# The second block's first feed-forward product, both token halves in seven products per 2x2x2 block

## The chip, the cores and the metric

The kernel runs on one core of a Trainium2 chip. The metric is device time in microseconds (us), from runs without a profiler; besides, one execution is recorded by the hardware profiler. Engines: TensorE (PE, with its weight loads PEld), VectorE (DVE), ScalarE (ACT), GpSimd (POOL), and SyncE (SP), which issues the DMAs.

## The reference

A trunk of two layers over 1024 tokens of width 1024, in float32. Each layer is a token mixer and a dense feed-forward block, each followed by a normalisation:

```
h = layer_norm(sqrt(2) * h + mixer(h))               # layer 0: RWKV-7, layer 1: S5 and a gate
h = layer_norm(sqrt(2) * h + square(relu(h @ w1)) @ w2)   # w1: 1024 x 4096, w2: 4096 x 1024
```

The S5 mixer is a diagonal complex state-space scan over all tokens; its output y goes through GELU and the gate z = y @ w_glu, z[:, :1024] * sigmoid(z[:, 1024:]).

## The kernel before

Activations are kept transposed: eight tiles of 128 features x 512 tokens for each half of the tokens, `hA` (first) and `hB` (second). A float32 product is done in three: each operand is split into a high part (fp32r, a cast on ScalarE) and the remainder (a subtraction on VectorE; `split`, L151 and L152), and high x high, high x low and low x high are added up in PSUM (`mm3`, issued at L197). Weights come by `wload` (L172): a raw tile of 256 KB by DMA (tag `wraw`, 2 buffers), split into `whi` and `wlo` (3 buffers each). PSUM tiles of products come from `psd` (tag `d`, 3 buffers).

The feed-forward block, `mlp`, treats the 4096 hidden features in 16 pairs of blocks of 128. `up(b)` computes a pair: for each of the two blocks 8 x 3 matmuls of 128x128 by 128x512, then ReLU on ScalarE (L985), the square on GpSimd (L986) and a split into `qbuf`. `down(b)` multiplies the pair by its rows of w2 (four weight tiles, 16 x 3 matmuls) and adds the eight results into h on VectorE (L1000 for the first pair, L1002 after). `up` runs one pair ahead of `down`. Each half has its own pass, so every weight is loaded and split once per half. In the last pass, the last TB = 2 pairs' `down` is done in two column halves, so that the last normalisation (`last_norm`) can start on one.

`layer_norm` sums over features with a matmul by a constant matrix, squares on ScalarE, adds on VectorE and GpSimd, and rescales. It uses temporary tiles of tags `la` and `m` (2 buffers each). `s5(H, h)` transposes its half, multiplies by tables to get the scan's inputs (`hb`), scans on VectorE and GpSimd (`advance`: L1232 to L1238, the groups 0 to 15 on VectorE, 16 to 31 on GpSimd where the step is long), multiplies by output tables (`tt`, `tcm`, tag `tab`, 4 buffers, loaded from DRAM), and writes y to DRAM through one buffer `yg`. `glu(H, h)` reads it back (`yload`, tag `m`), and does two products of 8 x 3 matmuls for each of eight feature tiles.

The order of the work: the program text gives each instruction a rising priority number, `rank(n)` sets it for a passage (smaller is more urgent; normalisations have 99000, S5 99300 and 99400, all else from 200000 up). A planner with a modelled time line then writes out the order on each engine. The passes stand in the program thus: feed-forward of layer 0 for hA; normalisation and S5 of hA; feed-forward of layer 0 for hB, with the gate of hA and its normalisation put in after INS3 = 12 pairs; normalisation and S5 of hB; feed-forward of layer 1 for hA, with the gate of hB and its normalisation put in after INS2 = 13 pairs; the last normalisation of hA and its store; feed-forward of layer 1 for hB, with the last normalisation.

The program's functions that the change touches, and their callers:

## Time and profile before

| | us |
|---|---|
| median of 3 runs | 2686.01 (2684.6 to 2688.53) |
| profiled execution, span from first to last instruction | 2674.1 |
| median less span | 11.9 |
| TensorE busy in the span | 2516.9 (94%) |
| VectorE, ScalarE, GpSimd busy | 1795.2, 1150.5, 578.8 |

The profile's rows name a line, an engine, an operation, and the output and inputs by tile name. Matmuls are pipelined: one of 128x512 is shown as some 390 ns long, but they start every 0.23 us in a dense stretch, so counts of matmuls over a stretch tell more than busy time. A few matmul records can be missing. In tables by stretch the columns are the stretch, its length, busy time and count for each engine, the granted TensorE clock (1.00 is full), the DMA engines' busy share and GB/s; in groups, the busy time and the mean of one in ns, then the idle time of the engine before them and what ended it.

### The profile page before, as it was taken

What the parts mean: (1) busy time and instruction counts of PE and PEld (TensorE: products, weight loads), DVE (VectorE), ACT (ScalarE), POOL (GpSimd) and SP (SyncE); (2) the same over time, 40 slices, a digit from 0 to 9 for tenths busy, and PEclk for the clock granted to TensorE, in tenths of its full rate; (3) what the DMA queues carried; (4) which work ended last, traced back from release to release, by engine and by line L of the source; (5) the groups of instructions that cost most, each with busy time, mean ns of one, the idle gap of its engine ahead of it and who ended that gap; (6) DMA issues with size and microseconds to landing.
All of it is one profiled execution on the core that took longest, in us unless ns stands there. A gap on an engine that the chain in (4) does not pass through costs nothing.

```text
span 2674.1 us, 44098 instructions
## 1 busy us (share of the span) xinstructions
PE 2516.9 (94%) x16768; PEld 2036.1 (76%) x16768; DVE 1795.2 (67%) x3140; ACT 1150.5 (43%) x2059; POOL 578.8 (22%) x484
## 2 busy tenths in 40 slices
PE   7899979999889999999998999999999999999997
PEld 5678757788667777777877788778778887788886
DVE  7367687487886867987586553675955536855556
ACT  7555565454454343344523332445233324533334
POOL 3121552342442122112121000121210001200001
PEclk9999889898889999999999999999999999999999
DMA  4765545663323334662436332234253322333333
GB/s 155 253 207 188 161 163 177 196 187 123 96 72 92 95 91 148 180 192 85 124 101 202 114 96 98 83 91 129 89 197 99 99 95 83 122 99 95 99 95 103
DMA packets 221397, 345.92 MB, mean 129 GB/s; under 512 B 21889, under 2 KB 83457, under 8 KB 221185
## 3 DMA queue, kind: packets, MB, share of 16 engines
q1 hardware_dynamic: 221184, 343.11, 41.4%
q8 instruction: 132, 2.16, 0.3%
q14 instruction: 81, 0.66, 0.1%
HBM read 279.06 MB, written 63.96 MB: 128 GB/s over the span
## 4 chain that ended last, share of the span: by engine, by line
PE 50%; DVE 13%; DMA 5%; issue 3%; ACT 2%; POOL 1%; SPq 0%; ACTq 0%; DVEq 0%; POOLq 0%
PE d L197 46%; DVE wlo L152 3%; DMA wraw<-in_mw_dram 2%; DMA s_y<-yg 1%; DVE hA L1002 1%; DMA yl<-s_y 1%; DVE t L1234 1%; DVE sq L887 1%; DVE hB L1002 1%; PE pbu L1222 1%; PE pu L1210 1%; DVE qbuf L152 1%; ACT whi L151 1%; DVE hb L1238 0%; POOL rl L986 0%
## 5 line engine op out<-in xcount | busy, mean ns | idle before, releaser
L151 ACT CAST whi<-wraw 128x512 fp32r<-128x512 f32 x668 | 413.7, 620 | 933.5 <-PE d L197 597.2
L152 DVE TENSOR_TENSOR wlo<-wraw,whi 128x512 fp32r<-128x512 f32 x668 | 500.9, 751 | 417.8 <-ACT whi L151 412.0
L197 PE MATMUL d<-qbuf,whi 128*128 128x512 f32 (+1 forms) x2112 | 655.8, 393 | 34.0 <-DVE hA L1002 14.1
L197 PEld LDWEIGHTS d<-qbuf,whi 128*128 128x128 f32 x2112 | 390.3, 190 | 132.0 <-DVE hA L1002 22.3
L197 PE MATMUL d<-qbuf,wlo 128*128 128x512 f32 (+1 forms) x1056 | 409.2, 390 | 9.2 <-DVE wlo L152 9.0
L197 PE MATMUL d<-oAh,whi 128*128 128x512 f32 (+1 forms) x960 | 385.3, 408 | 12.0 <-ACT ev L427 8.3
L986 POOL TENSOR_TENSOR rl<-rl 128x512 f32<-128x512 f32 x128 | 148.9, 1163 | 1135.3 <-ACT rl L985 1130.5
L197 PE MATMUL d<-oAl,whi 128*128 128x512 f32 (+1 forms) x960 | 380.9, 400 | 8.0 <-DVE oAl L152 8.0
L197 PE MATMUL d<-oAh,wlo 128*128 128x512 f32 (+1 forms) x960 | 381.9, 402 | 2.8 <-DMA wlo<-low 2.8
L197 PE MATMUL d<-oBh,whi 128*128 128x512 f32 x704 | 278.6, 396 | 1.9 <-ACT whi L151 1.9
L197 PE MATMUL d<-oBh,wlo 128*128 128x512 f32 x704 | 277.7, 395 | 1.9 <-DVE wlo L152 1.9
L197 PE MATMUL d<-oBl,whi 128*128 128x512 f32 x704 | 275.2, 391 | 0.0
L197 PEld LDWEIGHTS d<-qbuf,wlo 128*128 128x128 f32 x1056 | 200.7, 190 | 55.0 <-DVE wlo L152 13.5
L197 PEld LDWEIGHTS d<-oAh,whi 128*128 128x128 f32 (+1 forms) x960 | 183.4, 193 | 55.0 <-ACT ev L427 10.4
L197 PEld LDWEIGHTS d<-oAl,whi 128*128 128x128 f32 (+1 forms) x960 | 183.6, 193 | 46.3 <-DVE oAl L152 9.9
L197 PEld LDWEIGHTS d<-oAh,wlo 128*128 128x128 f32 (+1 forms) x960 | 183.2, 192 | 43.1 <-DMA wlo<-low 3.0
L1002 DVE TENSOR_TENSOR hB<-hB,d 128x512 f32<-128x512 f32 (+1 forms) x256 | 165.0, 652 | 62.0 <-PE d L197 59.3
L1002 DVE TENSOR_TENSOR hA<-hA,d 128x512 f32<-128x512 f32 x240 | 162.3, 684 | 53.0 <-PE d L197 50.4
L197 PEld LDWEIGHTS d<-oBh,wlo 128*128 128x128 f32 x704 | 132.2, 188 | 34.0 <-DVE wlo L152 3.2
L197 PEld LDWEIGHTS d<-oBh,whi 128*128 128x128 f32 x704 | 132.4, 188 | 30.2 <-ACT whi L151 2.9
L197 PEld LDWEIGHTS d<-oBl,whi 128*128 128x128 f32 x704 | 132.2, 188 | 29.3 <-issue 0.7
L152 DVE TENSOR_TENSOR qbuf<-rl,qbuf 128x512 fp32r<-128x512 f32 x128 | 96.5, 754 | 70.8 <-ACT qbuf L151 70.1
(365 smaller groups left out, 3629.7 us busy)
## 6 DMA issues: line engine op xcount, KB each, us to landing
wraw<-in_mw_dram SPq DMA_DIRECT2D x520, 256.0 KB, 2.7
wraw<-in_glu_dram SPq DMA_DIRECT2D x64, 256.0 KB, 2.6
low<-wlo SPq DMA_DIRECT2D x52, 256.0 KB, 2.8
wlo<-low SPq DMA_DIRECT2D x52, 256.0 KB, 3.6
wraw<-in_wk_dram SPq DMA_DIRECT2D x32, 256.0 KB, 3.2
wraw<-in_wr_dram SPq DMA_DIRECT2D x32, 256.0 KB, 3.8
wraw<-in_wv_dram SPq DMA_DIRECT2D x32, 256.0 KB, 4.6
yl<-s_y SPq DMA_DIRECT2D x32, 256.0 KB, 3.4
```

The lines of the kernel that those rows point to most:

```text
L151: S.copy(hi, src)
L152: (e or V).tensor_sub(lo, src, hi.bitcast(F32))
L197: bulk.append((PE.matmul(p, w, x, **kw).ins, x.shape[-1]))
L887: (G if k % 2 else V).tensor_add(sa[k % 2], sa[k % 2], q)
L986: G.tensor_mul(r, r, r)
L1002: V.tensor_add(z, z, p)
L1210: PE.matmul(p[64 * (1 - e) : 64 * (1 - e) + 64, g], u1[:, j, g].rearrange("p s c -> p (s c)"), sel[:, e], start=True, stop=True)
L1222: PE.matmul(p[qs, g2, ri], tb[:, g2, ri, qs], u[:, 2 * g2 + par], start=True, stop=True)
L1234: e.tensor_mul(t2[:, :, ri], x[:, :, 1 - ri], bw[:, l, g0:g1, ri : ri + 1].broadcast_to([128, g1 - g0, n]))
```

## The change

In layer 1 the two token halves are taken through 13 of the 16 pairs together. With K the two halves of the 1024 input features, M the two blocks of a pair and N the two token halves, a pair's first product is a 2x2x2 block product; Strassen's scheme (in Winograd's form) does it in seven products of 4 x 3 matmuls in place of eight. The token operands T1 to T4 are sums of quarters of hA and hB, made and split once, and kept in a new pool `jp`, which takes the space of S5's pool (closed after the second S5), and in buffers of `qbuf` and of hA's operands. The weight sums (s1, s2 and two more) are made for each pair on GpSimd from four raw tiles (two of tag `wraw`, two of tag `m`); the results are put together from PSUM on VectorE, ScalarE and GpSimd. `down` then uses each weight tile for both halves.

The first JB = 3 pairs are done for hA alone before that (`blocks`, the former body of `mlp`), and for hB alone after it, the last two of them with `down` in two column halves as before. The gate of hA is moved behind the whole of hB's feed-forward pass of layer 0, and the gate of hB follows it, ahead of all of layer 1's feed-forward work. Manual dependences hold the raw tiles of tag `m` back until the last token sum is done (`after`), and the first joint pair's tiles of tag `wraw` until the last weight load before them (`behind`). Nothing else of the computation changes.

```diff
 TB = 2
+JB = 3
...
             PE.transpose(out, x, idt)
 
+    behind = []
...
         for k0 in range(0, kt, step):
             kept = low.get((key, k0)) if key else None
             raw = wp.tile([128, step, n], F32, tag="wraw", name="wraw", bufs=2)
-            SP.dma_start(raw, src[:, k0 : k0 + step])
+            behind.append(SP.dma_start(raw, src[:, k0 : k0 + step]))
             hi = wp.tile([128, step, n], F32R, tag="whi", name="whi")
             lo = wp.tile([128, step, n], F32R, tag="wlo", name="wlo")
             nw[0] += 1
...
             hs.append(h)
         return hs
 
-    def mlp(i, H, h, xo):
-        nb = 32 // KB2
+    def blocks(i, h, xo, qbuf):
+
         nw = 512 // KB2
         qs = {}
 
...
                 split(r, qt[:, 0], qt[:, 1])
                 qs[b].append((qt[:, 0], qt[:, 1]))
 
-        def down(b, cs=slice(0, HT)):
+        def down(b, first=False, cs=slice(0, HT)):
             for n2 in range(C // nw):
                 w = wload(A["mw2"][i, b, n2], KB2, nw)
                 for n in range(nw // 128):
...
                     dense(p, [(x[:, n * 128 : (n + 1) * 128], y[:, n * 128 : (n + 1) * 128]) for x, y in w],
                           [(x[:, cs], y[:, cs]) for x, y in qs[b]])
                     z = h[n2 * (nw // 128) + n][:, cs]
-                    if b == 0:
+                    if first:
                         V.scalar_tensor_tensor(z, z, ALPHA, p, op0=ALU.mult, op1=ALU.add)
                     else:
                         V.tensor_add(z, z, p)
+
+        return up, down
+
+    def mlp(i, h, xo, qbuf):
+
+        nb = 32 // KB2
+        up, down = blocks(i, h, xo, qbuf)
         up(0)
-        last = TB if i == 1 and H == 1 else 0
-        for b in range(nb - last):
+        for b in range(nb):
             if b + 1 < nb:
                 up(b + 1)
-            down(b)
+            down(b, b == 0)
             yield
-        if last:
-            for b in range(nb - last + 1, nb):
-                up(b)
-            for c in range(2):
-                for b in range(nb - last, nb):
-                    down(b, slice(256 * c, 256 * c + 256))
-                yield
+
+    def both(i, hP, hQ, P, Q, tops, first, after):
+
+        nw = 512 // KB2
+        P1, P2, Q2 = P[0:4], P[4:8], Q[4:8]
+        T1, T2, T3, T4 = tops
+        qs = {}
+
+        def raw(pool, tag, f, k0):
+            t = pool.tile([128, 4, 128], F32, tag=tag, name="raw", bufs=2)
+            d = SP.dma_start(t, A["mw1"][i, f][:, k0 : k0 + 4])
+            if pool is tp or f < 2 * first + 2:
+                tc.add_manual_dep(d.ins, (after if pool is tp else behind[-1]).ins.name, mybir.DependencyInfo(
+                    mybir.DependencyClass.Sync, mybir.DependencyReason.DATA), reason="order")
+            return t
+
+        def weights(t):
+            hi = wp.tile([128, 4, 128], F32R, tag="whi", name="whi")
+            lo = wp.tile([128, 4, 128], F32R, tag="wlo", name="wlo")
+            split(t, hi, lo)
+            return hi, lo
+
+        def product(p, t, xs, add=False):
+            hi, lo = weights(t)
+            for k in range(4):
+                for j, (w, x) in enumerate(((hi, xs[k][0]), (hi, xs[k][1]), (lo, xs[k][0]))):
+                    PE.matmul(p, w[:, k], x, start=not add and k + j == 0, stop=k == 3 and j == 2, skip_group_check=True)
+
+        def ev(name):
+            return tp.tile([128, HT], F32, tag="ev", name=name, bufs=EVB)
+
+        def power(dst, x):
+            S.activation(dst, x, AF.Relu)
+            G.tensor_mul(dst, dst, dst)
+            qh, ql = (jp.tile([128, HT], F32R, tag=nm, name=nm, bufs=6) for nm in ("qh", "ql"))
+            split(dst, qh, ql)
+            return qh, ql
+
+        def up(b):
+            f1, f2 = 2 * b, 2 * b + 1
+            r11, r12 = raw(wp, "wraw", f1, 0), raw(wp, "wraw", f1, 4)
+            r21, r22 = raw(tp, "m", f2, 0), raw(tp, "m", f2, 4)
+            s1, s2 = (tp.tile([128, 4, 128], F32, tag="la", name=nm, bufs=2) for nm in ("s1", "s2"))
+            G.tensor_add(s1, r21, r22)
+            G.tensor_sub(s2, s1, r11)
+            pa_ = psd()
+            product(pa_, r11, P1)
+            m1 = ev("m1")
+            S.copy(m1, pa_)
+            pb_ = psd()
+            product(pb_, s2, T2)
+            V.tensor_add(m1, pb_, m1)
+            product(pa_, r12, P2, True)
+            r = ev("rl")
+            c1 = power(r, pa_)
+            G.tensor_sub(r21, r11, r21)
+            pc_ = psd()
+            product(pc_, r21, T3)
+            u3 = ev("u3")
+            V.tensor_add(u3, pc_, m1)
+            pd_ = psd()
+            product(pd_, s1, T1)
+            m5 = ev("m5")
+            S.copy(m5, pd_)
+            G.tensor_sub(s2, r12, s2)
+            pe_ = psd()
+            product(pe_, r22, T4)
+            G.tensor_add(m5, m5, u3)
+            V.tensor_sub(u3, u3, pe_)
+            product(pd_, s2, Q2, True)
+            V.tensor_add(m1, pd_, m1)
+            c2, c4, c3 = power(u3, u3), power(m5, m5), power(m1, m1)
+            qs[b] = (c1, c2), (c3, c4)
+
+        def down(b):
+            for n2 in range(C // nw):
+                w = wload(A["mw2"][i, b, n2], KB2, nw)
+                for n in range(nw // 128):
+                    for h, q, fresh in ((hP, qs[b][0], b == first), (hQ, qs[b][1], False)):
+                        p = psd()
+                        dense(p, [(x[:, n * 128 : (n + 1) * 128], y[:, n * 128 : (n + 1) * 128]) for x, y in w], q)
+                        z = h[n2 * (nw // 128) + n]
+                        if fresh:
+                            V.scalar_tensor_tensor(z, z, ALPHA, p, op0=ALU.mult, op1=ALU.add)
+                        else:
+                            V.tensor_add(z, z, p)
+
+        return up, down
 
     def glu(H, h):
         ys = yload(H)
...
 
     aw = sp.tile([128, 4, 32, 2], F32, name="aw")
     bw = sp.tile([128, 4, 32, 2], F32, name="bw")
-    qbuf = ap.tile([128, 2 * KB2, 2, HT], F32R, tag="q", name="qbuf", bufs=1)
+    def qtile():
+        return ap.tile([128, 2 * KB2, 2, HT], F32R, tag="q", name="qbuf", bufs=1)
+
+    NB = 32 // KB2
     tc.cur_priority = 200000
+    qbuf = qtile()
     hA, xo = first_out
-    ma = mlp(0, 0, hA, xo)
+    ma = mlp(0, hA, xo, qbuf)
     for _ in range(INS1):
         next(ma)
     hB = wo(1)
...
     with tc.tile_pool(name="pp", bufs=1) as pp:
         with rank(S5R):
             s5_tables()
-    s5p = ctx.enter_context(tc.tile_pool(name="s5p", bufs=1))
+    sctx = ctx.enter_context(ExitStack())
+    s5p = sctx.enter_context(tc.tile_pool(name="s5p", bufs=1))
     with rank(99000):
         layer_norm(hA, 1, 0, False)
     with rank(99300):
         s5(0, hA)
-    mb = mlp(0, 1, hB, xoB)
-    for _ in range(INS3):
-        next(mb)
-    glu(0, hA)
-    with rank(99000):
-        xo = layer_norm(hA, 2, 0)
-    run(mb)
+    run(mlp(0, hB, xoB, qbuf))
     with rank(99000):
         layer_norm(hB, 1, 1, False)
     with rank(99400):
         s5(1, hB)
-    ma = mlp(1, 0, hA, xo)
-    for _ in range(INS2):
-        next(ma)
+    sctx.close()
+    jp = ctx.enter_context(tc.tile_pool(name="jp", bufs=1))
+    glu(0, hA)
+    with rank(99000):
+        xo = layer_norm(hA, 2, 0)
+    t3 = []
+    for k in range(4):
+        t = jp.tile([128, HT], F32, tag="qh", name="t3", bufs=6)
+        G.tensor_sub(t, hA[k + 4], hA[k])
+        t3.append(t)
     glu(1, hB)
     with rank(99000):
         xoB = layer_norm(hB, 2, 1)
-    run(ma)
+
+    ua, da = blocks(1, hA, xo, qbuf)
+    ua(0)
+    for b in range(JB - 1):
+        ua(b + 1)
+        da(b, b == 0)
+    tops = [[], [], [], []]
+    t3b = qtile()
+    with rank(99100):
+        for k in range(4):
+            a = tp.tile([128, HT], F32, tag="m", name="ta")
+            V.tensor_sub(a, xo[k][0].bitcast(F32), hB[k])
+            V.tensor_add(a, a, xo[k][1].bitcast(F32))
+            d = [jp.tile([128, HT], F32R, tag="t1", name="t1", bufs=8) for _ in range(2)]
+            split(a, *d)
+            tops[0].append(d)
+            a = tp.tile([128, HT], F32, tag="m", name="tb")
+            G.tensor_add(a, t3[k], hB[k])
+            d = [jp.tile([128, HT], F32R, tag="t2", name="t2", bufs=8) for _ in range(2)]
+            split(a, *d)
+            tops[1].append(d)
+            after = G.tensor_sub(a, a, hB[k + 4])
+            tops[3].append(operand(a))
+        for k in range(4):
+            d = t3b[:, k, 0], t3b[:, k, 1]
+            split(t3[k], *d)
+            tops[2].append(d)
+    uj, dj = both(1, hB, hA, xoB, xo, tops, JB, after)
+    da(JB - 1, JB == 1)
+    uj(JB)
+    for b in range(JB + 1, NB):
+        uj(b)
+        dj(b - 1)
+    qbuf = qtile()
+    ub, db = blocks(1, hB, xoB, qbuf)
+    ub(0)
+    dj(NB - 1)
     with rank(99000):
         layer_norm(hA, 3, 0, False)
     store(0, hA)
-    mb = mlp(1, 1, hB, xoB)
-    for _ in range(32 // KB2 - TB + 1):
-        next(mb)
-    with rank(LN8R):
-        last_norm(hB, 3, 0)
-    run(mb)
+    for b in range(JB - TB):
+        ub(b + 1)
+        db(b)
+    for b in range(JB - TB + 1, JB):
+        ub(b)
+    for c in range(2):
+        for b in range(JB - TB, JB):
+            db(b, False, slice(256 * c, 256 * c + 256))
+        if c == 0:
+            with rank(LN8R):
+                last_norm(hB, 3, 0)
     with rank(99000):
         last_norm(hB, 3, 1)
     if PACE:
```

## The prediction, made before the result was known

> **What bounds the kernel now.** I read the page's totals first, then a table by stretches.
>
> ```profile
> span 2674.1 us, 44098 instructions
> PE 2516.9 (94%) x16768; PEld 2036.1 (76%) x16768; DVE 1795.2 (67%) x3140; ACT 1150.5 (43%) x2059; POOL 578.8 (22%) x484
> ```
>
> ```profile
> core 0: us, PE busy (x) PEld busy (x) DVE busy (x) ACT busy (x) POOL busy (x), PEclk, DMA share, GB/s
> 1605.00:1692.00 87.00, 87.00 (x386) 71.99 (x385) 35.02 (x53) 23.84 (x41) 7.56 (x10) 1.00 0.30 97
> 2003.00:2145.00 142.00, 141.78 (x626) 117.05 (x625) 77.78 (x119) 45.52 (x78) 13.19 (x13) 1.00 0.32 97
> 2350.00:2600.00 250.00, 250.00 (x1096) 205.42 (x1095) 132.50 (x202) 80.45 (x139) 24.10 (x23) 1.00 0.32 97
> ```
>
> TensorE is the bound in a plain stage (1096 matmuls fill 250 us, 0.228 us each, at clock 1.00); no other engine is near. So fewer matmuls are time saved, as long as TensorE has other work during the serial parts. The first row is the gate (glu) of the first half; the rows after it are feed-forward work.
>
> The serial part that matters is the second half's normalisation and S5 mixer, from the last product of block 0 (1774.8) to the last operand of the gate.
>
> ```profile
> 1774.26 1.41 DVE L1002 TENSOR_TENSOR hB<-hB,d 128x512 f32<-128x512 f32 x2
> 2002.94 0.69 DVE L152 TENSOR_TENSOR oBl<-yl,oBh 128x512 fp32r<-128x512 f32 x1 [1.34 <-ACT oBh L151]
> ```
>
> That is 228.8 us. The same table for the dense products alone (tile d) shows what TensorE did meanwhile, and at two later places:
>
> ```profile
> 1774.80:2003.00 228.20, 172.92 (x705) 0.99 0.41 133
> 1689.70:1774.80 85.10, 78.51 (x334) 1.00 0.28 84
> 2226.00:2290.00 64.00, 58.60 (x246) 1.00 0.28 80
> ```
>
> At 0.228 us these are 160.7, 76.2 and 56.1 us of dense work: 67.5, 8.9 and 7.9 us were something else, the mixer's own matmuls or idle.
>
> **The products.** For two feature blocks and both halves, the first product takes 96 matmuls now and 7 x 4 x 3 = 84 after. Thirteen pairs save 156, at 0.228 us: **-35.6 us**.
>
> What the other engines get in such a pair (180 matmuls, 41.0 us):
>
> ```profile
> L152 DVE TENSOR_TENSOR wlo<-wraw,whi 128x512 fp32r<-128x512 f32 x53 | 36.5, 689 | 38.4 <-ACT whi L151 38.2
> L1002 DVE TENSOR_TENSOR hA<-hA,d 128x512 f32<-128x512 f32 x53 | 36.3, 687 | 15.9 <-PE d L197 14.9
> L986 POOL TENSOR_TENSOR rl<-rl 128x512 f32<-128x512 f32 x128 | 148.9, 1163 | 1135.3 <-ACT rl L985 1130.5
> ```
>
> VectorE: 11 weight splits and 4 operand splits at 0.689, 16 adds into h and 4 combinations at 0.687, 24.1 us (before, 16 splits of weights and no combinations: 24.8). GpSimd: 4 squares and 5 sums at 1.163, 10.5 us. ScalarE some 21 instructions of about 0.62, 13 us. Half the first weights' loads and half the second's go. All of it lies under 41.0. Between two of the seven products stand 2.7 us of TensorE, and three PSUM buffers rotate through five accumulators, but the one that is added to later has a product in between. I put **+3 us** for the stage, with bounds 0 (all hidden) and 26 (2 us per pair, a weight tile late behind its GpSimd sum).
>
> One rule speaks against this. The Trainium skill's page "SBUF — State Buffer" (its single rule on contention) has GpSimd and a two-input VectorE instruction hold one port exclusively, the other waiting for the whole instruction. By it the 10.5 us of GpSimd would all go onto VectorE, 34.6 us, still under 41.0; the sum would not move, only the chance of the rival below.
>
> **What else moves.** The first half's gate no longer stands inside block 0's last pairs, but behind them, and the second half's S5 is no longer under 13 pairs of feed-forward work: only the first half's gate (384 matmuls, 87.6 us) precedes the second half's gate. Could TensorE go on with the first half's three feed-forward pairs, which come later in the program? The order of the weight loads says no:
>
> ```profile
> L172 SPq DMA_DIRECT2D wraw<-in_wv_dram x16: 328/382/829, 510.3 to 601.0; - x16
> L172 SPq DMA_DIRECT2D wraw<-in_wo_dram x16: 327/333/1001, 603.5 to 682.4; - x16
> L172 SPq DMA_DIRECT2D wraw<-in_glu_dram x3: 328/328/328, 1592.1 to 1597.8; - x3
> ```
>
> wo's weights carry the more urgent rank (99000 against 100000) and need no data, yet they are fetched after the last of wv, which stands earlier in the program; the gate's came at 1592, when their turn was, though its operands were done at 1486:
>
> ```profile
> L151 ACT CAST oAh<-yl x16: 603/619/622, 606.1 to 1486.0; 128x512 fp32r<-128x512 f32 x16
> ```
>
> Buffers of one tag are handed out in program order. So the second gate's first weights sit in the two raw and three split buffers until S5 delivers, and TensorE waits. By the same order the first gate's inputs (tag m) stand behind the squares of the normalisation ahead of them, so TensorE also waits at the start of the chain; that only changes where the hole is.
>
> How long is the chain then? Four stages: normalisation to 1813.4, transposes and inputs to 1867.7, scan to 1939.6 (from there the output of the lower groups can start), output to 2003.6.
>
> ```profile
> 1867.70:1939.60 71.90, 65.22 (x287) 50.95 (x286) 67.43 (x113) 17.22 (x29) 17.51 (x10) 0.95 0.31 99
> ```
>
> *Normalisation*, 38.6 now. Its own instructions:
>
> ```profile
> L879 DVE TENSOR_TENSOR hB<-hB,pm 128x512 f32<-128x512 f32 x8 | 4.9, 683 | 0.0
> L887 DVE TENSOR_TENSOR sq<-sq,sq 128x512 f32<-128x512 f32 x3 | 4.0, 1326 | 0.0
> L894 POOL TENSOR_TENSOR rs<-rs,mhalf 128x4 f32<-128x4 f32 x1 | 1.4, 1394 | 1.5 <-DVE rs L893 1.5
> ```
>
> With sums and their matmuls (about 4), the reciprocal's spread (2) and the first products, that is 19; without feed-forward work between, 22 (20 to 38.6).
>
> *Inputs*, 54.3 now: four rounds, with dense products and weight casts between.
>
> ```profile
> 1815.55 1.05 ACT L1204 COPY u<-pu 128x512 f32<-128x512 f32 x2
> 1856.15 0.59 ACT L1204 COPY u<-pu 128x512 f32<-128x512 f32 x1 [0.97 <-PE pu L1203]
> ```
>
> Three rounds in 40.6 us. The gate still runs beside the last ones: 49 (42 to 54.3).
>
> *Scan*, 71.9. VectorE is nearly full in it (67.4); its scan instructions, from 1864 on, and GpSimd's part ahead of them:
>
> ```profile
> L1234 DVE TENSOR_TENSOR t<-hb,bw 128x32 f32<-128x32 f32 (+2 forms) x27 | 13.2, 528 | 0.0
> L1238 DVE TENSOR_TENSOR hb<-hb,t 128x64 f32<-128x64 f32 (+2 forms) x14 | 11.0, 784 | 0.2
> L1232 DVE TENSOR_TENSOR t<-hb,aw 128x64 f32<-128x64 f32 (+2 forms) x13 | 10.5, 804 | 0.1
> L1236 DVE TENSOR_TENSOR t<-t,t 128x64 f32<-128x64 f32 (+2 forms) x14 | 8.0, 574 | 0.2
> ...
> 1867.74 1.95 POOL L1232 TENSOR_TENSOR t<-hb,aw 128x1024 f32<-128x1024 f32 x1 [4.90 <-DVE hb L1238]
> 1875.13 2.45 POOL L1238 TENSOR_TENSOR hb<-hb,t 128x1024 f32<-128x1024 f32 x1
> ```
>
> 42.7, less some 2.5 before 1867.7, plus 9.9 of GpSimd: 50 alone. The remainder, 22, is feed-forward work cutting in. The gate loads VectorE 35.0/87 = 0.40 where feed-forward loads it 77.8/142 = 0.55, and ends during the scan: 12 instead of 22, so 62 (52 to 71.9).
>
> *Output*, 64.0. SP's queue stood before the tables of the second round, behind a weight load that waited for its buffer:
>
> ```profile
> 1943.59 0.42 SPq L1258 DMA_DIRECT2D tcm<-tC  x1
> 1949.56 1.78 SPq L172 DMA_DIRECT2D wraw<-in_mw_dram  x2
> 1951.39 0.42 SPq L1256 DMA_DIRECT2D tt<-tT  x1
> ```
>
> In the hole no weights pass by there; I take off 6 for this round and as much for the later ones together: 52 (46, or 64 if the first half's normalisation, which now falls here with the more urgent rank, takes it back).
>
> The sum is 185 us (160 to 228.8). The gate can begin some 4 us before its last operand (its first 24 matmuls run 5.5 us): 181, less its sister's 87.6, leaves 93.4 that is not dense work, against 67.5: **+25.9**. TensorE comes out of the hole slow:
>
> ```profile
> 740.00:745.00 5.00, 2.43 (x15) 2.22 (x12) 4.94 (x9) 4.95 (x8) 0.00 (x0) 0.50 0.00 0
> ```
>
> At half clock for a few microseconds, **+2** (0 to 5). The first half's second normalisation falls into the hole, so its 8.9 is returned: **-8.9**.
>
> **The token sums.** T1 to T4 cost VectorE 8 sums and 16 splits, 16.5 us, behind the second half's normalisation and beside the first half's last pairs, where VectorE has little room; and the first pair's weights are fetched only behind them (a load 2.7, two GpSimd sums, a split: 6). I take **+10** (0 if the 54.7 us of those pairs hide it; 22 if nothing does). At the end three pairs still cover the first half's last normalisation (240 matmuls, 54.7 us, against the 38.6 of the stage above): nothing; uncovered it would be some 20.
>
> Sum: -35.6 + 25.9 + 2 - 8.9 + 10 + 3 = **-3.6 us**. The profiled execution has a span of 2674.1; the median of the runs, 2686.0, is 11.9 above it. So 2670.5 in the profile and **2682 us** in the runs.
>
> **The rivals.**
> *The chain stays as long as it is* (slower). If its stages take 228.8 as now, because the order on each engine is fixed and the first half's normalisation cuts in, the chain term is 69.7 instead of 25.9: +40.2, 2726. For it: VectorE's 67.4 of 71.9. Against: half of the other load is gone by then. It decides from a chain of 194.
> *The first half's feed-forward pairs fill the hole* (faster). If buffers are given to whatever is ready, five half-steps (54.7 us) go into the hole at some 10 us of lengthening: chain term -18.8; but then normalisation and token sums stand bare, 22 + 21 less the last 10.9, +24 over now instead of +10; the clock stays up. -35.6 - 18.8 - 8.9 + 24 + 3 = -36, 2650. Against it: the order of the weight loads.
> *The seven products don't run back to back*: the 26 in place of 3, 2705. Against: every other engine is below 60% of the pair. It would show as idle time before each product.
>
> **How the numbers follow.** Forecast 0.52, with its own range 2664 to 2700; chain as long 0.18; filled 0.18; products late 0.12. About 0.2%, 5 us, can be told from no change. The forecast's spread puts 0.23 below, 0.19 within, 0.10 above; with the rivals faster 0.41, same 0.20, slower 0.39. The range 2652 to 2718 leaves out the far ends of the second and third.
>
> **What would show it.** Right: 156 matmuls fewer; one or two holes between 1690 and 1880 with about 45 us more idle TensorE than now, glu's first weights loaded well ahead of its first matmul, clock 0.5 there; the joint stage at 0.228 per matmul. Wrong: feed-forward weights of the first half loaded before the second gate's; a chain above 194; idle time of over 1 us per joint pair.

## The result, and the profile after

The changed kernel takes **2735.33 us** (2731.28 to 2741.26, 4 runs) where the kernel before takes 2687.27 us (2684.6 to 2690.16, 4 runs): a ratio of **1.018**, 95% interval 1.0161 to 1.0199. The forecast was 2682, the range 2652 to 2718. The change makes the kernel slower by 48 us.

The totals of the page of after; the matmul count (x) is 156 below that of before, as designed:

```profile
span 2739.5 us, 43555 instructions
...
PE 2520.2 (92%) x16612; PEld 2033.7 (74%) x16612; DVE 1826.9 (67%) x3151; ACT 1139.3 (42%) x2036; POOL 696.9 (25%) x561
```

Of the two profiled executions, the part ahead of the change must be set aside first. The order of the instructions is the same on every engine up to the second half's layer-0 feed-forward pass, and yet its first add into `hB` came at 1281.2 us in before and at 1298.7 in after (the views of that tile, before and then after; first and last start in us):

```profile
L1000 DVE SCALAR_TENSOR_TENSOR hB<-hB,d x16: 680/682/691, 1281.2 to 2328.3; 128x512 f32<-128x512 f32 x16
```

```profile
L1002 DVE SCALAR_TENSOR_TENSOR hB<-hB,d x8: 677/679/681, 1298.7 to 1311.6; 128x512 f32<-128x512 f32 x8
```

From this add to the end of the span, before has 1392.9 us and after 1440.8: **+47.9**, which is what the runs show. All that follows is counted from there. The tables by stretch, for the dense products alone (tile `d`), before and then after; the figure in brackets is their matmul count:

```profile
1281.20:1774.80 493.60, 429.75 (x1813) 340.07 (x1814) 91.16 (x135) 21.34 (x36) 0.99 0.36 115
2003.00:2560.00 557.00, 549.52 (x2390) 447.03 (x2389) 119.04 (x175) 29.63 (x50) 1.00 0.32 98
2560.00:2674.10 114.10, 89.41 (x462) 74.87 (x460) 27.48 (x54) 3.56 (x6) 0.94 0.33 100
```

```profile
1298.70:1689.30 390.60, 337.96 (x1428) 267.40 (x1428) 85.96 (x127) 16.60 (x28) 0.99 0.38 118
1689.30:2003.30 314.00, 194.81 (x771) 148.60 (x771) 11.28 (x18) 9.49 (x16) 0.87 0.33 108
2003.30:2120.00 116.70, 98.16 (x402) 76.62 (x401) 19.42 (x30) 5.88 (x10) 0.94 0.23 71
2120.00:2640.00 520.00, 520.00 (x2270) 426.15 (x2269) 173.02 (x255) 21.62 (x37) 1.00 0.17 52
2640.00:2739.50 99.50, 65.96 (x342) 53.44 (x340) 19.20 (x42) 2.36 (x4) 0.90 0.35 106
```

Each stretch, less 0.228 us for each matmul, leaves the time in which TensorE did no dense work or did it at a lower clock (the last stretch of either kernel holds 192 half-width matmuls, counted as 96):

| us that are not dense work | before | after | difference | forecast |
|---|---|---|---|---|
| layer-0 pass of the second half | 80.2 | 65.0 | -15.2 | -8.9 |
| from its last product to the end of the second gate | 67.5 | 138.2 | **+70.7** | +27.9 |
| next normalisation, in after with the token sums | 7.9 | 25.0 | +17.1 | +10 |
| from there to the end stretch | 4.2 | 2.4 | -1.8 | +3 |
| end stretch | 30.7 | 43.4 | +12.7 | 0 |

(In before the chain is counted to the gate's last operand, by the prediction's row; the gate itself lies in the dense stretch from 2003. Its 7.9 is from the prediction's stretch 2226 to 2290, taken out of the 12.1 of that long stretch.) That is +83.5; 157 recorded matmuls fewer are -35.8, together +47.7. The products gave what they should. Most of the loss is in the chain of S5.

The chain in after, as rows of the timeline (start, length, engine, line), from the last layer-0 product at 1689.3 on:

```profile
1720.36 0.75 PE L1292 MATMUL pu<-ident,hB 128*128 128x128 f32 x4
...
1773.69 0.59 ACT L1312 COPY hb<-pbu 128x512 f32<-128x512 f32 x1 [0.35 <-PE pbu L1311]
...
1834.36 1.23 DVE L1327 TENSOR_TENSOR hb<-hb,t 128x1024 f32<-128x1024 f32 x1
...
1841.50 2.71 DVE L877 TENSOR_TENSOR sa<-sa,sb 128x512 f32<-128x512 f32 x1
...
1886.10 2.08 PE L879 MATMUL pm<-sa,ones_c 128*128 128x512 f32 x2 [3.26 <-DVE yg L1376]
1888.21 4.87 DVE L881 TENSOR_TENSOR hA<-hA,pm 128x512 f32<-128x512 f32 x8 [2.17 <-PE pm L879]
...
1896.37 19.18 SPq L959 DMA_DIRECT2D yl<-s_y  x8
...
1922.20 1.77 DVE L153 TENSOR_TENSOR oBl<-yl,oBh 128x512 fp32r<-128x512 f32 x1
```

Normalisation takes 31 us (to 1720.4), inputs 54 (to 1774.3), the scan 61 (to 1835.6), the output 88 (to 1924.0). The forecast had 22, 49 and 62 for the first three; the output was to take 52. The last of its eight `yg` was done at 1886.0, and the gate read the first one back only at 1896.4. From the last `yg` to the gate's last operand 38 us passed, where before took 8.2 (its `yg` are shown further down):

```profile
L1376 DVE SCALAR_TENSOR_TENSOR yg<-hB,pv,pyt x8: 1128/1142/1173, 1846.0 to 1884.9; 128x512 f32<-128x512 f32 x8
```

The rows between tell why. The first half's second normalisation (`sa`) had its sum by 1844.2, but its first matmul (`pm`) ran at 1886.1, released by the last `yg`: `pm` and S5's `pyt` share the one PSUM bank of tag `l`, and the bank is handed out in program order. The squares of that normalisation hold tag `m`, the gate's `yl` stands behind them, and so reading y back began at 1896.4. TensorE meanwhile (dense products in 20 us each, clock in the third column from the end):

```profile
1820.00:1840.00 20.00, 10.24 (x36) 7.40 (x34) 1.37 (x2) 0.59 (x1) 0.83 0.21 69
1840.00:1860.00 20.00, 0.00 (x0) 0.00 (x0) 0.00 (x0) 0.00 (x0) 0.72 0.61 208
1860.00:1880.00 20.00, 0.00 (x0) 0.00 (x0) 0.00 (x0) 0.00 (x0) 0.68 0.42 145
1880.00:1900.00 20.00, 0.40 (x1) 0.40 (x2) 0.00 (x0) 0.00 (x0) 0.57 0.15 53
```

### The profile page after: what moved, and what is told of

The parts are those of the page before. It is cut to its first block, busy times and chain, and to the rows that moved or that the text cites. A ratio compares the mean times of both kernels' runs of the same rounds, so it can differ in the third digit from the quotient of the medians.

```text
span 2739.5 us, 43555 instructions
## 1 busy us (share of the span) xinstructions
PE 2520.2 (92%) x16612; PEld 2033.7 (74%) x16612; DVE 1826.9 (67%) x3151; ACT 1139.3 (42%) x2036; POOL 696.9 (25%) x561
## 4 chain that ended last, share of the span: by engine, by line
PE 61%; DVE 18%; DMA 9%; ACT 5%; issue 4%; POOL 2%; SPq 1%; ACTq 0%; DVEq 0%; POOLq 0%
PE d L199 43%; PE d L1044 9%; DVE wlo L153 3%; DMA wraw<-in_mw_dram 1%; DMA wraw<-in_wr_dram 1%; DVE oAl L153 1%; ACT whi L152 1%; DMA yl<-s_y 1%; DMA wraw<-in_wo_dram 1%; PE py L1356 1%; DVE t L1323 1%; DVE hA L1004 1%; DVE KB L578 1%; PE pu L1299 1%; PE pbu L1311 1%
## 5 line engine op out<-in xcount | busy, mean ns | idle before, releaser
L152 ACT CAST whi<-wraw 128x512 fp32r<-128x512 f32 x512 | 316.9, 620 | 744.6 <-PE d L199 421.9
L153 DVE TENSOR_TENSOR wlo<-wraw,whi 128x512 fp32r<-128x512 f32 x512 | 407.3, 797 | 290.2 <-ACT whi L152 284.9
L199 PE MATMUL d<-qbuf,whi 128*128 128x512 f32 (+1 forms) x1280 | 393.7, 391 | 23.5 <-DVE hA L1004 8.3
L199 PEld LDWEIGHTS d<-qbuf,whi 128*128 128x128 f32 x1280 | 234.5, 191 | 84.2 <-DVE hA L1004 14.1
L199 PE MATMUL d<-qbuf,wlo 128*128 128x512 f32 (+1 forms) x640 | 245.6, 388 | 7.1 <-DVE wlo L153 6.9
L199 PE MATMUL d<-oBh,whi 128*128 128x512 f32 x496 | 198.2, 402 | 16.6 <-ACT oBh L152 11.4
L199 PE MATMUL d<-oBh,wlo 128*128 128x512 f32 x496 | 198.2, 401 | 3.4 <-DVE wlo L153 3.4
L199 PEld LDWEIGHTS d<-oAl,whi 128*128 128x128 f32 (+1 forms) x752 | 145.6, 195 | 41.0 <-DVE oAl L153 12.1
L199 PE MATMUL d<-qh,wlo 128*128 128x512 f32 x416 | 164.0, 394 | 0.0
L199 PE MATMUL d<-ql,whi 128*128 128x512 f32 x416 | 163.2, 392 | 0.0
L199 PE MATMUL d<-qh,whi 128*128 128x512 f32 x416 | 161.7, 389 | 0.0
```

The source lines that it names most:

```text
L152: S.copy(hi, src)
L153: (e or V).tensor_sub(lo, src, hi.bitcast(F32))
L199: bulk.append((PE.matmul(p, w, x, **kw).ins, x.shape[-1]))
```

## The experiments

All versions were timed beside the kernel before on the same chip (its medians were 2686 to 2690 us in these series). "From the first add" is the span behind the marker above, in the one profiled execution. Set against before, it and the medians differ by up to 9 us for one version, so smaller differences between versions are weak.

| version | median, us | ratio to before, 95% | from the first add |
|---|---|---|---|
| after | 2735.33 | 1.0180 (1.0161 to 1.0199) | 1440.8 |
| new order, plain products | 2731.34 | 1.0161 (1.0135 to 1.0187) | 1442.3 |
| normalisation behind the second gate | 2713.68 | 1.0101 (1.0068 to 1.0135) | 1425.2 |
| normalisation with other PSUM | 2714.58 | 1.0102 (1.0067 to 1.0138) | 1421.0 |
| four pairs at either end | 2719.72 | 1.0118 (1.0088 to 1.0148) | 1429.6 |
| eight products in the joint pairs | 2756.27 | 1.0268 (1.0242 to 1.0293) | 1465.2 |
| second sums in tag la | 2725.90 | 1.0150 (1.0131 to 1.0169) | 1437.2 |
| dense work ahead of the second gate: 8, 4 | 2713.11 | 1.0104 (1.0072 to 1.0135) | 1422.3 |
| the same: 7, 4 | 2724.48 | 1.0145 (1.0119 to 1.0171) | 1434.1 |
| the same: 9, 5 | 2712.58 | 1.0095 (1.0064 to 1.0127) | 1423.6 |
| before's order, 4 joint pairs | 2693.24 | 1.0033 (1.0017 to 1.0050) | 1404.8 |
| before with INS2 = 8, none joint | 2692.81 | 1.0013 (0.9996 to 1.0029) | 1399.5 |
| before's order, 5 joint pairs, sums late | 2701.74 | 1.0053 (1.0033 to 1.0073) | 1410.9 |

My theory after the result: the new order costs more than the products save. The rival: the order is nearly free, and the joint stage eats the saving.

**The order alone.** The new order, then plain passes of 16 pairs:

```diff
     glu(0, hA)
     with rank(99000):
         xo = layer_norm(hA, 2, 0)
-    (token sums, joint pairs)
     glu(1, hB)
     with rank(99000):
         xoB = layer_norm(hB, 2, 1)
+    run(mlp(1, hA, xo, qbuf))
+    (last normalisation and store of hA, 16 pairs for hB)
```

> The order of the changed kernel alone: the gate of hA behind layer 0's feed-forward passes, the gate of hB behind S5, then two plain passes of 16 pairs in layer 1; no token sums, no seven products. The whole result is computed. Theory (the loss is the chain from hB's normalisation to its gate, which the new order lays bare): in the changed kernel 314.0 us pass from the end of layer 0's last product (1689.3) to the end of the second gate (2003.3), 175.1 of them dense; that is 71 us more bare time than before, of which 15 come back in layer 0's pass. So before + 56, less nothing for the products: 2687 + 56 = 2743, range 2733 to 2750. Rival (the loss is in the joint stage, its sums and its end; the order is nearly free): within 10 us of before, 2680 to 2697.

The order alone costs 41 us of the median, so the rival falls. The theory had 56; the median is just under its range of 2733 to 2750. Its stretches of dense products, normalisation (no sums) and end:

```profile
1677.00:1986.40 309.40, 193.63 (x780) 147.50 (x779) 11.92 (x19) 9.51 (x16) 0.88 0.33 110
1986.40:2090.00 103.60, 99.71 (x433) 80.62 (x432) 21.29 (x33) 5.90 (x10) 1.00 0.30 91
...
2600.00:2728.90 128.90, 102.28 (x517) 85.30 (x515) 28.77 (x56) 4.74 (x8) 0.93 0.33 98
```

Not dense: 131.6 in the chain, 4.9, and 32.9 at the end. After has 138.2, 25.0 and 43.4 there: 37.2 more, as much as its products save. So in this order the joint form gains nothing, and the loss beside it is the chain's, 131.6 against 67.5.

**Who holds the second gate back.** Two versions take the first half's second normalisation out of the way, one by place, one by PSUM.

```diff
     glu(0, hA)
+    glu(1, hB)
     with rank(99000):
         xo = layer_norm(hA, 2, 0)
     (differences of the first half's tokens)
-    glu(1, hB)
```

> The changed kernel with one passage moved: the second normalisation of hA stands behind the second gate in the program, no longer ahead of it. Theory (buffers are handed out in program order, so reading y back waits for the squares of that normalisation, tag m, which in turn waits for S5's last transposes in the one PSUM bank of tag l): y is read back as it is written, from about 14 us after the scan, and the last operand of the gate is there some 27 us sooner; the normalisation then runs beside the gate and costs about 7 there. 2735 - 20 = 2715, range 2705 to 2722. Rival (the output stage is bound by its own loads and by the single buffer of y): no change, 2730 to 2740.

```diff
-            return pl.tile([128, HT], F32, tag="l", name=name)
+            return bank() if bank else pl.tile([128, HT], F32, tag="l", name=name)
...
-        xo = layer_norm(hA, 2, 0)
+        xo = layer_norm(hA, 2, 0, bank=psd)
```

> The changed kernel with one thing exchanged: the three PSUM tiles of hA's second normalisation come from the products' ring (tag d) and not from the bank (tag l) that S5's last transposes use. The order of the program is kept, so y still stands behind the normalisation's squares. Theory (the bank is what holds the normalisation, and with it y): its first PSUM product starts at about 1844 on the time line of the changed kernel, right behind its sum, instead of 1886; y is read back from about 1858; 2735 - 22 = 2713, range 2705 to 2722. Rival (the normalisation is late for another reason, its place in TensorE's queue or its rank): the same as the changed kernel, 2730 to 2740.

Both took some 21 us off the median, as foretold. With the program's order kept and only the bank changed, the matmul of the sum runs as soon as the sum is there, and y is read back from 1840 on (timeline of the version with other PSUM; then the row of `yg` from that tile's view, and the chain's stretch of dense products):

```profile
1819.25 1.22 DVE L1327 TENSOR_TENSOR hb<-hb,t 128x1024 f32<-128x1024 f32 x1
...
1829.15 2.08 PE L879 MATMUL d<-sa,ones_c 128*128 128x512 f32 x2 [4.98 <-DVE sa L877]
...
1846.67 1.13 DVE L1376 SCALAR_TENSOR_TENSOR yg<-hB,pv,pyt 128x512 f32<-128x512 f32 x1 [2.04 <-DMA s_y<-yg]
...
1854.94 4.87 DVE L904 TENSOR_TENSOR hA<-hA,d 128x512 f32<-128x512 f32 x8 [1.85 <-PE d L901]
1859.73 1.18 DVE L1376 SCALAR_TENSOR_TENSOR yg<-hB,pv,pyt 128x512 f32<-128x512 f32 x1
...
1892.81 1.09 DVE L153 TENSOR_TENSOR oBl<-yl,oBh 128x512 fp32r<-128x512 f32 x1 [3.79 <-ACT oBh L152]
```

```profile
L1376 DVE SCALAR_TENSOR_TENSOR yg<-hB,pv,pyt x8: 1123/1164/1282, 1836.1 to 1885.1; 128x512 f32<-128x512 f32 x8
```

```profile
1675.10:1969.40 294.30, 195.22 (x792) 146.80 (x793) 21.52 (x34) 9.51 (x16) 0.92 0.35 116
```

So the shared bank is shown to be the holder. In this row 14 of the 792 matmuls are the normalisation's own; with 778 dense ones 116.9 us are left, so the bank is worth 21.3 of the chain's 138.2. But the output stage came down to 73 us (1820.5 to 1893.9), not to 52: the eight `yg` take 49.0 us from first to last start where after took 38.9. The normalisation's work cuts in between two of them, 13 us apart. That isn't all of it: with the normalisation behind the second gate, where none of it stands between them, they take 49.4. In both versions y is read back and the gate begins between the `yg`, in after not; which step of that stretches them isn't shown. Before, which reads y back there too, took 43.3 (that tile's view):

```profile
L1287 DVE SCALAR_TENSOR_TENSOR yg<-hB,pv,pyt x8: 1128/1190/1296, 1950.9 to 1994.2; 128x512 f32<-128x512 f32 x8
```

**Cover for the token sums.** Four separate pairs at either end:

```diff
-JB = 3
+JB = 4
```

> The changed kernel with JB = 4: four pairs for each half alone, 12 joint. Theory (the token sums, 24 us of bare time between the second gate and the joint stage, and the end, 12 us more bare time than before, lack cover): one more pair is 43.8 us of cover at either place, at 12 matmuls more, 2.7 us; the token sums keep some 8 us as the normalisation had before, the end loses its 12: 2735 + 3 - 16 - 10 = 2712, range 2705 to 2725. Rival (they are bound by what they wait for, and more pairs don't help): 2738, range 2733 to 2743.

It fell between the theory's 2712 and the rival, within the range, 15.6 us faster though it saves 2.7 us fewer products.

**Where the sums wait.** Behind the second gate of after, TensorE waits 11.5 us in one piece for the first weight sum of the joint stage to be split. GpSimd's eight steps of the sums are spread from 2038 to 2087 us, and the joint stage's first weight sum follows the last of them (timeline of after, first and last step):

```profile
2038.43 1.32 POOL L1449 TENSOR_TENSOR tb<-t,hB 128x512 f32<-128x512 f32 x1 [4.67 <-DMA wraw<-in_mw_dram]
...
2085.70 1.26 POOL L1453 TENSOR_TENSOR tb<-tb,hB 128x512 f32<-128x512 f32 x1 [4.83 <-DVE t L153]
2091.52 1.26 POOL L1061 TENSOR_TENSOR s<-raw 128x512 f32<-128x512 f32 x1 [4.56 <-DMA raw<-in_mw_dram]
```

```diff
-            a = tp.tile([128, HT], F32, tag="m", name="tb")
+            a = tp.tile([128, HT], F32, tag="la", name="tb", bufs=2)
```

> The changed kernel with one word changed: the second kind of token sum takes its buffers from the normalisation's tag (la, two buffers) and no longer shares tag m's two with the first kind. Theory (the eight sums go through one ring of two buffers, a round of 10 to 12 us each, and the joint stage's first weights wait for the last): 5 to 12 us less, 2727 (2722 to 2731), and the last sum about 10 us earlier behind the normalisation. Rival (VectorE's own queue of splits sets the pace): 2735, the last sum where it was.

The last step now starts 68 us behind the second gate's last add (2059.8 and 1992.2), in after 81 (2085.7 and 2004.4). The median is 9.4 lower, as the theory has it. The profile gives less: the stretch has 21.4 us that are not dense, against 25.0. The two agree on the sign only, so the size is not settled.

**What the seven products are worth.** The joint stage with eight:

```diff
-            (four raw tiles, sums s1 and s2, seven products, recombination)
+            for n in range(KB2):
+                w = wload(A["mw1"][i, b * KB2 + n], KT, 128)
+                for j, xs in enumerate((P, Q)):
+                    p = psd()
+                    dense(p, w, xs)
```

> The changed kernel, but the joint stage's first product goes back to eight plain products per block (192 matmuls in the two halves of a pair where the seven take 168); the order, the first three token sums and the three separate pairs at either end stay. The fourth token sum is left out of the operands, as nothing reads it. Theory (the matmuls saved are worth their 0.228 us in full, the loss is all in the order): 156 matmuls more, 2735 + 35.6 = 2771 (2763 to 2777; a few us less if the fourth sum's split was on the path). Rival (the seven products cost idle time that offsets a part of the saving): under 2760.

The median rose by 21 (24 by the ratios), not by 35.6, below the rival's mark. A first form, which still made operands of the fourth sum that nothing read, gave no time. But the profile speaks against the rival's mechanism. The joint stage, and the stretch of the sums ahead of it, in this version; then the sums' stretch with JB = 4 and with tag `la`:

```profile
1990.30:2090.00 99.70, 89.81 (x370) 69.71 (x369) 16.59 (x25) 5.34 (x9) 0.97 0.24 74
2120.00:2640.00 520.00, 520.00 (x2272) 426.32 (x2271) 133.90 (x195) 27.41 (x46) 1.00 0.16 49
```

```profile
1998.70:2120.00 121.30, 110.83 (x464) 87.92 (x463) 23.28 (x36) 6.48 (x11) 0.97 0.26 81
```

```profile
1992.20:2110.00 117.80, 102.32 (x423) 80.33 (x422) 20.11 (x30) 6.47 (x11) 0.97 0.23 72
```

520 us hold 2272 matmuls with eight products and 2270 with seven: not one of the seven's matmuls is late, so 35.6 is their worth there. Most of the shortfall is ahead of the stage: plain weights don't wait for the last token sum, and with the fourth sum's split gone 15.3 us are not dense, against 25.0 (with JB = 4, 15.5). I had left this wait out of the expectation.

**Filling the hole.** If program order keeps feed-forward work out of the hole, dense work put ahead of the second gate should fill it. The first half's gate goes ahead of the normalisation and S5, then its normalisation (with other PSUM) and four or five of its pairs, then the second gate:

```diff
     run(mlp(0, hB, xoB, qbuf))
+    glu(0, hA)
     with rank(99000):
         layer_norm(hB, 1, 1, False)
     with rank(99400):
         s5(1, hB)
-    glu(0, hA)
     with rank(99000):
-        xo = layer_norm(hA, 2, 0)
+        xo = layer_norm(hA, 2, 0, bank=psd)
+    ua, da = blocks(1, hA, xo, qbuf)
+    (four or five pairs)
     glu(1, hB)
```

> A version made to beat both: the first half's gate stands ahead of the second half's normalisation and S5 mixer in the program, the first half's second normalisation takes its PSUM from the ring of three, four of the first half's feed-forward pairs stand ahead of the second gate, and eight pairs of 16 are joint-free (so 8 are joint, five fewer than in the changed kernel). The differences of the first half's tokens are taken from its operands, not from the stream. Theory (buffers are handed out in program order, and dense work that stands ahead of the second gate fills its chain): from the changed kernel's 2735, five joint pairs fewer +14, time in the chain that is not dense 138 to 50-70 (-70 to -90), token sums 25 to 15 (-9), the end covered by more pairs (0 to -11): 2655 (2640 to 2675). Rival A (the chain grows by as much as dense work is put under it, to 250 or more): 2685 to 2700. Rival B (the pairs do not start before the second gate): over 2715.

> The same with seven joint-free pairs (9 joint) and four of them ahead of the second gate, so that two pairs instead of three lie over the token sums. Theory: 2.7 less for the ninth joint pair, but the token sums stick out 7 to 9 more, as in the changed kernel: 2659 (2644 to 2680), 3 to 7 above the version with eight. Rival (the sums are hidden by two pairs as well): 3 below the version with eight.

> The same with nine joint-free pairs (7 joint) and five of them ahead of the second gate. If the chain of the second half is still open when four pairs are done, the fifth takes 22 us of it and costs 2.7: up to 19 below the version with eight. If four pairs fill it: 3 above. Theory: chain 210 to 235 against a gate of 88, four pairs of 88 and some 35 of the mixer's own matmuls and the normalisation, 211, so 0 to 15 below.

All three came out far above the forecast of some 2655: 2713, 2724, 2713. Rows of the first (8, 4): the chain from the last product to the gate's last operand, and two pieces of it; then the sums' stretch of this version and of that with 7:

```profile
1690.00:1926.20 236.20, 150.86 (x601) 112.45 (x600) 21.30 (x34) 7.71 (x13) 0.90 0.35 116
1800.00:1840.00 40.00, 10.51 (x38) 7.23 (x37) 8.86 (x16) 0.00 (x0) 0.60 0.08 27
1860.00:1900.00 40.00, 15.21 (x61) 10.63 (x59) 1.28 (x2) 1.79 (x3) 0.91 0.69 230
...
2073.20:2190.00 116.80, 103.27 (x417) 78.19 (x416) 23.65 (x36) 5.29 (x9) 0.97 0.24 75
```

```profile
2079.20:2190.00 110.80, 82.63 (x332) 62.32 (x331) 18.73 (x28) 4.12 (x7) 0.91 0.19 60
```

The pairs do start ahead of the gate (not rival B), and the chain is as long as after's, 236 (not rival A, which had it at 250). Yet 102.4 us of it are not dense (14 of the 601 matmuls are the normalisation's own), 34.9 more than in before. The first half's normalisation stands bare (1800 to 1840): TensorE waits 7.6 us for its sum, 12.9 for its squares, 3.9 for its scale and 8.1 for the first operands behind it, while VectorE, which has the scan to do as well, is busy 39.4 of these 40 us. The stretch beside S5's output (1860 to 1900) is not what is new: it gets 61 matmuls in 40 us, and before's own (1940 to 1980) gets 68. TensorE is not starved there; it waits 5.8 us and is busy 34.2, 19 of that with S5's own small matmuls. The fifth pair, expected to bring 0 to 15 us, brought 0.5 by the median. With 7, two pairs instead of three lie over the sums, 35.1 us are not dense against 21.7: 13.4 more, 2.7 less for the ninth joint pair, and the median is 11.4 higher. That part of the expectation had the right sign and was too small.

**Before's order with joint pairs at its end.** Four joint pairs; then, as the control, the kernel before with the same number of the first half's pairs ahead of the second gate; then five joint pairs with the sums at a later turn. In the joint ones the differences of the first half's tokens are made from its operands, by three GpSimd sums each. The order up to the second gate is before's; beside that, against after:

```diff
-INS2 = 13
+INS2 = 8
...
-JB = 3
+JB = 12
```

> The order of before as far as the second gate (the first half's gate inside the first block's last pairs, the second half's mixer under feed-forward pairs of the first half), with eight such pairs ahead of the second gate where before has thirteen, four more behind it over the token sums, and the last four pairs joint. Theory (the joint products are sound, the loss is in the order): from before's 2687, four joint pairs -11, token sums +4 (0 to 8), chain 0 to +6 as before's 705 matmuls in the chain are 7.3 pairs: 2681 (2676 to 2692). Rival (joint pairs cost as much as they save wherever they stand): 2688 or more.

> The kernel before with one number changed: eight feed-forward pairs of the first half ahead of the second gate instead of thirteen, no joint products. The control for the version with four joint pairs. Theory (before's chain of 228.8 us holds 7.3 pairs, so eight are cover enough): 2687 (2683 to 2692). Rival (the gate's weights or inputs come in its way earlier): 2693 or more.

```diff
-JB = 12
+JB = 11
...
-    with rank(99100):
-        (token sums)
+    (token sums, without a rank of their own, second kind in tag la)
```

> The version with before's order and joint pairs at the end, changed in three ways: five joint pairs instead of four (three pairs lie over the token sums), the token sums take their turn behind the feed-forward pairs' work instead of ahead of it (their more urgent rank is taken away), and their second kind uses the normalisation's buffers. Theory (in the version with four, VectorE made TensorE wait because sums and splits were put ahead of the adds that empty PSUM): joint pairs -13.7, sums +4 to +8, control +3: 2681 (2675 to 2689) where before has 2686. Rival (16 us of VectorE work for the sums costs TensorE as much wherever it stands in the order): 2690 or more.

The control is before within what can be told (0.9996 to 1.0029), its median just over the expected range. Both joint versions came out above theirs. Four joint pairs are slower than before by 0.17 to 0.50%. They are 5.3 us longer than the control from the first add, 0.4 by the medians, though they have 10.9 us of products less: 11 to 16 us go elsewhere. The control from the last operand to past its normalisation; the sums' stretch with four joint pairs, and from the view of waits what TensorE waited for in 2130 to 2300 (us, times, longest); the same two views with five (waits in 2130 to 2320):

```profile
2010.00:2250.00 240.00, 233.51 (x1014) 189.20 (x1013) 41.31 (x61) 12.43 (x21) 1.00 0.29 93
```

```profile
2130.10:2290.00 159.90, 147.42 (x610) 114.77 (x609) 37.49 (x56) 7.62 (x13) 0.98 0.23 69
```

```profile
PE d L199 <- DVE hA L1004: 7.3, 6, 2.0
```

```profile
2140.00:2240.00 100.00, 80.99 (x309) 60.40 (x308) 18.78 (x28) 3.54 (x6) 0.93 0.21 62
```

```profile
PE d L199 <- DVE hA L1004: 10.5, 8, 2.5
```

Not dense: 8.8, 20.8, and 29.5. About a third of that in either joint version is TensorE waiting for VectorE's adds out of PSUM. With five pairs and the later turn the median meets the rival's mark (2690 or more), but three things were changed at once, so what the place of the sums does by itself isn't shown. No version beats the kernel before.

## Why the prediction was wrong

**The chain of S5 is the step that failed**, +25.9 and +2 in the sum, +70.7 measured. Within it the *output* stage did: I took off 12 us for weight loads that no longer pass SP's queue and got 52, with 64 as the bound "if the first half's normalisation takes it back". It took 88, and 30 of the 36 over lie between the last `yg` and the gate's last operand (38 us where before had 8.2). I had used the rule "buffers of one tag are handed out in program order" for the first gate's inputs behind the second half's squares, and did not apply it once more: the second gate's inputs stand behind the first half's squares, and these behind S5's last transposes, through a PSUM bank of one buffer. Other PSUM took 21.3 us off the chain's bare time. Of the 12 us at most 4.4 were there: first to last `yg` took 43.3 in before and 38.9 in after, where neither feed-forward weights nor reads of y stand in SP's queue between them; in the two versions above, with reads but no such weights, it took 49.0 and 49.4. So the queue's stop at the tables was a small part of what paced the stage. What else does stays open. In after, between 1836 and 1886, TensorE waited 7.8 us for tables `tt` and 7.5 for S5's `y` from ScalarE. Of the eight `yg` of after, three waited for the write of the one before out of the single buffer and five for the transposes (that tile's view: us in all, times); a second buffer wasn't tried.

```profile
  PE pyt L1374: 23.6, 5
  DMA s_y<-yg: 9.1, 3
```

*Normalisation* and *inputs*, 31 and 54, were 14 over my 22 and 49, inside their bounds; the *scan*, 62 by subtracting the other work from VectorE, measured 61, though the two terms of that subtraction were not measured apart. The chain of 234.7 is past the 194 that I named as a sign of being wrong.

**The rival "the chain stays as long as it is"** had the right length, 234.7 against 228.8, and the price 2726 was 9 short. That it came so near is in part luck. Its reason, a fixed order and the normalisation cutting in, is half of what happened: the normalisation did lengthen the chain, but by holding the reads of y back through the bank, and that was in none of my cases. "The first half's pairs fill the hole" is out, as the weight order said: after has 771 dense matmuls up to the end of the second gate, and the two gates alone have 768. The versions that forced such pairs in show that the normalisation which must come before them then lies bare.

**The products, -35.6, held**, and so did "all of it lies under 41.0": 2270 matmuls in 520.0 us are 0.229 each. All engines in the joint stage of after (stretch), and the slowest weight split in it (groups):

```profile
2120.00:2640.00 520.00, 520.00 (x2270) 426.15 (x2269) 310.22 (x446) 152.09 (x260) 130.07 (x108) 1.00 0.17 52
```

```profile
L153 DVE TENSOR_TENSOR wlo<-wraw,whi 128x512 fp32r<-128x512 f32 x58 | 53.2, 916 | 21.8 <-ACT whi L152 21.7
```

VectorE is busy 0.60 of the stage, my 24.1 of 41.0 being 0.59. The lock of the Trainium skill's "SBUF — State Buffer" (SBUF: two separate sides) was to make it 34.6 of 41.0, an estimate, and this trace doesn't show that. That page of the Trainium skill has the lock only where both of VectorE's inputs are in SBUF, and 20 of a pair's 35 VectorE instructions read PSUM, so the estimate charged too much. Something of the kind is there: these splits run 916 ns against 689 in before and those of `u` 1355, some 21 us more in the 520, while GpSimd is busy 130.1. With eight products, GpSimd busy 49.0, all splits stay at 0.69. TensorE loses nothing by it. "The products late" is out.

**The token sums**, +10 in the sum, cost 17 (bounds 0 and 22), and 20 against the same order without them. I had seen both parts, VectorE's 16.5 us and the first weights behind them, and split the difference.

**The end**, forecast at nothing, cost 12.7. Too little cover is the likely reason, since it shrinks with more separate pairs at the end: after (three) 43.4, the new order with four 38.8, before's order with twelve 32.4, before (sixteen) 30.7, all by the same count. The rows of the two new ones:

```profile
2600.00:2721.80 121.80, 91.39 (x460) 73.98 (x458) 26.35 (x54) 3.55 (x6) 0.94 0.35 106
```

```profile
2560.00:2692.30 132.30, 105.77 (x534) 88.31 (x532) 29.98 (x58) 4.74 (x8) 0.94 0.32 98
```

**What came back in layer 0** was 15.2, not 8.9. The first half's gate left this stretch too, likely with the other 6.3. The 11.9 us that I put between span and median are not time around the span. Each timed run is 1.7 to 2.1 above its span (2741.26 and 2739.5 in after); the profiled execution of before was a quick one.

## What to carry to other kernels

When a chain is uncovered, write down for every buffer and PSUM tag that its consumers use who stands ahead in program order, and follow that to the end: a single bank shared by two otherwise independent chains makes one wait for the whole of the other. A scheme that saves matmuls must be charged for the reordering that makes its operands available together: here the joint form saved 35.6 us, lost as much again, most of it to sums and thinner cover, and its order cost 41 on top. Rows show the price of such an order before it is built only if each uncovered stage is costed by what paced it, not by taking off what happened to stand beside it.

## What was not expected of the hardware

Executions of the same instruction order reached the same point, some 1290 us in, over a range of 17 us (1281.2 to 1298.7 in the profiles of before and after); a difference of a few us between two profiles must be counted from a common marker. In the hole of after the granted clock, as a mean over 20 us, went 0.83, 0.72, 0.68, 0.57, while little but S5's and the normalisation's small matmuls ran. These are not four clocks: by stretches of 2 us it stood at 0.50 or at 1.00, with values between only where it changed, and at 0.50 for a growing share of the time (all of 1884 to 1906).
